# Moving a kernel's SBUF tiles from 64 and 96 bytes past a multiple of 128 to the multiple itself

## The chip, the cores and the metric

The kernel runs on one core of a Trainium2 chip. The time is the device time of one execution in microseconds; three executions gave 1589.37, 1592.58 and 1593.47 us, so the median is 1592.58. SBUF is the on-chip memory with 128 partitions; a tile `[P, D]` of float32 takes D × 4 bytes in every partition, at one and the same byte address in each. TensorE multiplies a stationary operand, which it loads first, with a moving operand, which it streams; it reads both from SBUF and writes to PSUM. This document is about the byte addresses at which these operands begin.

## What is computed

One decoder block on x of 1024 tokens by 1024 channels (`seq` = `D_MODEL` = 1024, one layer, one batch element), in float32:

```python
u = rms_norm(h, norm_mix); proj = u @ w_in
u_ssm, q, k, v, f_logit, gate_logits = split(proj)
y_ssm = gelu(s5_ssm(u_ssm, ...))                  # diagonal state-space branch, 512 wide
out_a = glu_a * sigmoid(glu_b)                    # from y_ssm @ w_glu
att = forgetting_attention(q, k, v, f_logit + b_forget)   # 8 heads of 64, causal
out_b = att @ w_fox_o
h = h + (gate_a * out_a + gate_b * out_b) @ w_mix_out
h = h + memory_cross_attention(rms_norm(h), rms_norm(mem), ...)   # 4 heads, 256 memory tokens
f_a, f_b = split(rms_norm(h, norm_ffn) @ w_ffn_in)
h = h + (silu(f_a) * f_b) @ w_ffn_out             # hidden width 2816
return rms_norm(h, norm_final)
```

## The kernel before

Every large product is made of three TensorE products. A float32 matrix is split into a high part (a cast to `float32r`, by ScalarE) and a low part (the rest, by VectorE); `split` (line 177) does it, and `mm3` (line 166) multiplies high by high, high by low and low by high into one PSUM bank. A matmul here has up to 128 rows, a stationary operand of mostly 128 columns and a moving operand of mostly 512 columns (2048 bytes in each partition); each has its own load of the stationary operand ahead of it.

The stages follow each other in the program: `stage_in` (norms, transposes, keys and values of the memory, the state-space input; its order is the hand-written string `ORDER_IN`), `stage_ssm` (gate products with the state-space branch between them), `Fox.run` (attention over eight heads, with the projections of later heads and the gated linear unit's products put between its score and value matmuls by hand-written slot tables), and `stage_tail` (the output products, cross-attention, and the feed-forward part, where seven products of half-size blocks replace eight). The order of the instructions is the order in which this code is written; nothing is planned at run time.

What decides the addresses is the allocation of the tile pools. Pools are laid out one behind the other in the order in which they are opened, and a tile's size is rounded up to 32 bytes. In this order stand: a few constants, `const` (identity, `mhalf`, `junk`), `small` (statistics of a few bytes), `wpool` with the weights as loaded (`raw`, two slots of `RAW` floats) and split (`whi`, `wlo`, four slots each of `WSLOT` floats), `big` (16 slots of 4096 bytes: the activations that are streamed), and behind it, one after another in the same place, the pools of the stages: `ssm` with `xin` or `qp` behind it, then `sh` (slots `half` of 2048 and `tmp` of 4096 bytes) with `fox` or `st2` behind it. So one small tile near the start moves everything behind it.

Three sizes matter to the change. `RAW` = 1072 and `SLOT` = 1040 (lines 31 and 32); `raw` holds at most 4 × 264 = 1056 floats, and `SLOT` is the size of the four `vhi` tiles of attention (line 1434), which hold two key blocks of 8 heads × 65 columns = 1040 floats. `msk` (line 1247) is the last tile of the pool `ssm`, 64 bytes, and `bfb` (line 1464) is a tile of 8 floats in `fox`, ahead of the attention tiles `hb`, `tri`, `trk`, `num`, `rb` and `pl`.

Where the operands of the matmuls begin, as the built program before has it (bytes past a multiple of 128):

| tiles | role on TensorE | past a multiple of 128 |
| --- | --- | --- |
| `whi`, `wlo`, all of `big`, `sh`, `st2` | moving and stationary, nearly all matmuls from the state-space stage on | 64 |
| `mT` (`mh`, `ml`), `xt` in `stage_in` | moving for the memory keys, stationary for its values | 96 |
| `qp` (state-space tables) and `hb0` to `hb3`, `pl` in `fox` | both, attention heads of odd number | 96 |
| `raw` | not read by TensorE | 64 and 0 |
| `vhi` | stationary, 65 columns from every 260 bytes | every multiple of 4 |
| `ident` | moving operand of the transposes | 0 |

The 264-column weights of the value projection (`values_of_v`, line 1445) lie four behind each other in one `whi` slot, 1056 bytes apart, so they begin at 64, 96, 0 and 32 past a multiple of 128, in this order.

Of the kernel before, what the change touches and what calls it, by code (L numbers as in the profile page):

```python
# [9 lines left out]
F32 = mybir.dt.float32  # L10
F32R = mybir.dt.float32r
# [8 lines left out]
P = 128  # L20
# [4 lines left out]
NH = 8  # L25
# [2 lines left out]
MH = 4  # L28
FH = 2816
EPS = 1e-6  # L30
SLOT = 1040
RAW = 1072

WSLOT = 1088
NEG = -1.0e30
# [31 lines left out]
def f32(ap):  # L67
    return ap.bitcast(F32)


class Act:


    def __init__(self, pool, tag, bufs, nk, n, kg=2, name="a"):
        self.kg, self.width = kg, D // kg

        def mk(s):
            return [[pool.tile([P, D], F32R, tag=tag, bufs=bufs, name=f"{name}{s}{k}_{h}")
                     .rearrange("p (k c) -> p k c", k=kg)
                     for h in range(n // self.width)] for k in range(nk // kg)]  # L80

        self.hi, self.lo = mk("h"), mk("l")
# [23 lines left out]
class Shared:  # L106
# [5 lines left out]
    def tmp(self, name, dt=F32):  # L112
        return self.pool.tile([P, D], dt, tag="tmp", bufs=4, name=name)
# [5 lines left out]
class Block:  # L119
    BANKS = {"mm": 3, "sc": 2, "pv": 2, "misc": 1}  # L120

    def __init__(self, ctx, tc):
        self.tc, self.nc = tc, tc.nc
        nc = self.nc
        self.V, self.A, self.G, self.T, self.S = nc.vector, nc.scalar, nc.gpsimd, nc.tensor, nc.sync
        self.const = ctx.enter_context(tc.tile_pool(name="const", bufs=1))
        self.small = ctx.enter_context(tc.tile_pool(name="small", bufs=3))
        self.wpool = ctx.enter_context(tc.tile_pool(name="wpool", bufs=4))
        self.dram = ctx.enter_context(tc.tile_pool(name="dram", bufs=1, space=DRAM))
        self.psum = ctx.enter_context(tc.tile_pool(name="psum", bufs=2, space=PSUM))  # L130
        self.ident = self.const.tile([P, P], F32, name="ident")
        make_identity(nc, self.ident)
        self.mhalf = self.const.tile([P, 1], F32, name="mhalf")
        nc.vector.memset(self.mhalf, -0.5)
        self.junk = self.const.tile([P, 512], BF16, name="junk")
        self.nbank = 0


    def bank(self, tag=None):
# [8 lines left out]
    def wload(self, pieces, cols, pool_lo=False, behind=None):  # L148

        raw = self.wpool.tile([P, RAW], F32, tag="raw", bufs=2, name="raw")  # L150
        for off, shape, src in pieces:
# [182 lines left out]
def stage_in(B, xp, s5, x, mem, g_mix, g_kv, w_in, w_mem_kv, uT, u_d, kv_d):  # L334
# [41 lines left out]
    def wget(i):  # L376
# [4 lines left out]
        else:  # L381
            src = w_in[:, C_U + (i - 8) * P:C_U + (i - 7) * P]
        raw[i] = B.wpool.tile([P, RAW], F32, tag="raw", bufs=2, name="raw")[:, :D]
        S.dma_start(raw[i].rearrange("p (k c) -> p k c", k=D // src.shape[-1]),
# [113 lines left out]
def stage_tail(B, big, s2, sh, x, glu, aT, gate_d, kv_d, w_fox_o, w_mix_out, g_mq, w_mem_q, w_mem_o, g_ffn,  # L498
# [57 lines left out]
    def wslots(src, pool_lo):  # L556

        nk = src.shape[0] // P
        raw = B.wpool.tile([P, RAW], F32, tag="raw", bufs=2, name="raw")[:, :D]
        S.dma_start(raw.rearrange("p (k c) -> p k c", k=nk), src.rearrange("(k p) c -> p k c", p=P))  # L560
# [241 lines left out]
    def w_fetch(j):  # L802
        raws[j] = B.wpool.tile([P, RAW], F32, tag="raw", bufs=2, name="raw")[:, :D], tmp("rawb")
        for r_, c in zip(raws[j], (0, FH)):
            f = S.dma_start(r_.rearrange("p (k c) -> p k c", k=8),
                            w_ffn_in[:, c + j * P:c + (j + 1) * P].rearrange("(k p) c -> p k c", p=P))
        return f
# [303 lines left out]
class S5:  # L1111
# [51 lines left out]
    def prepare(self):  # L1163
        B, sp, cT, bb, dbc, par = self.B, self.sp, self.cT, self.braw, self.dbc, self.par
# [76 lines left out]
        for i in range(2):  # L1241
            G.memset(self.cb[i], 0.0)
            for g in range(2):
# [4 lines left out]
        G.memset(msk, 1.0)  # L1248
        G.affine_select(out=msk, in_=msk, pattern=[[-1, 16]], compare_op=ALU.is_equal, fill=0.0, base=-112,
                        channel_multiplier=1)  # L1250
        self.dm = dbc.rearrange("p (g m) -> p g m", g=GRP)
        V.tensor_tensor(out=self.dm, in0=self.dm,
                        in1=msk.unsqueeze(1).to_broadcast([P, GRP, 16]), op=ALU.mult)
# [165 lines left out]
class Fox:  # L1419
# [11 lines left out]
    def prepare_v(self):  # L1431

        fp, G = self.fp, self.B.G
        self.vh = [fp.tile([P, SLOT], F32R, tag="vhi", bufs=4, name="vhi").rearrange("p (k h d) -> p k h d", k=2, h=NH)
                   for _ in range(4)]
        self.vl = [fp.tile([P, D], F32R, tag="vlo", bufs=4, name="vlo").rearrange("p (k c) -> p k c", k=2)
                   for _ in range(4)]
        for v_ in self.vh:
            G.memset(f32(v_[:, :, :, 64:65]), 1.0)
        self.fl = self.sh.half("fl")[:, :NT * NH].rearrange("p (t h) -> p t h", t=NT)  # L1440
        self.wv = {}
        for b, (c0, n) in ((1, (256, 264)), (0, (0, 256))):
            self.wv[b] = [self.B.wblock(self.w_in, 4 * kk, 4, C_V + c0, n, behind=self.B.ordered) for kk in range(2)]
# [17 lines left out]

    def log_forget(self):
        B, fp, V, S = self.B, self.fp, self.B.V, self.B.S
        bfb = fp.tile([P, NH], F32, name="bfb")
        S.dma_start(bfb, self.b_forget.partition_broadcast(P))
        both = self.sh.half("logf"), self.sh.half("logf")
        tmp = [t_[:, 64 * i:64 * i + 64] for t_ in both for i in range(8)]
        xl, ax, ee, s_, s2 = tmp[:5]
        V.tensor_tensor(out=xl.rearrange("p (t h) -> p t h", t=NT), in0=self.fl,
                        in1=bfb.unsqueeze(1).to_broadcast([P, NT, NH]), op=ALU.add)  # L1470
        V.tensor_scalar(out=ax, in0=xl, scalar1=-1.0, scalar2=None, op0=ALU.mult)
        V.tensor_tensor(out=ax, in0=ax, in1=xl, op=ALU.min)
        pp, sc = B.exp_parts(lambda s: tmp[5 + "xc k r p ib".split().index(s)], ax)
        V.scalar_tensor_tensor(out=ee, in0=pp, scalar=1.0, in1=sc, op0=ALU.add, op1=ALU.mult)

        V.tensor_scalar(out=s_, in0=ee, scalar1=2.0, scalar2=None, op0=ALU.add)
        V.reciprocal(s_, s_)
        V.tensor_mul(s_, s_, ee)
        V.tensor_mul(s2, s_, s_)
        V.tensor_scalar(out=ee, in0=s2, scalar1=1.0 / 17, scalar2=None, op0=ALU.mult)  # L1480
        for d in (15, 13, 11, 9, 7, 5, 3):
            V.scalar_tensor_tensor(out=ee, in0=ee, scalar=1.0 / d, in1=s2, op0=ALU.add, op1=ALU.mult)
        V.scalar_tensor_tensor(out=ee, in0=ee, scalar=1.0, in1=s_, op0=ALU.add, op1=ALU.mult)
        V.tensor_scalar(out=xl, in0=xl, scalar1=0.0, scalar2=None, op0=ALU.min)
        V.scalar_tensor_tensor(out=xl, in0=ee, scalar=-2.0, in1=xl, op0=ALU.mult, op1=ALU.add)
        self.logf = xl
# [42 lines left out]
    def project(self, h):  # L1529
# [5 lines left out]
        def load(behind=None):  # L1535
            src = lambda c: self.w_in[:, c + h * DH:c + (h + 1) * DH].rearrange("(k p) c -> p k c", p=P)
            raw = self.raw[h] = B.wpool.tile([P, RAW], F32, tag="raw", bufs=2, name="raw")[:, :D]
            rv = raw.rearrange("p (k c) -> p k c", k=8)
# [272 lines left out]
```

## Time and profile before

| | |
| --- | --- |
| time of an execution, median of 3 (lowest to highest) | 1592.58 us (1589.37 to 1593.47) |
| span of the profiled execution, first to last instruction | 1586.7 us |
| around the span, taken as median less span | 5.9 us |
| mean granted TensorE clock | 0.988 |
| matmuls | 7313, of which 5,844 with 512 columns |
| TensorE busy | 97% of the span |
| VectorE, ScalarE, GpSimd busy | 64%, 41%, 16% |
| DMA, mean | 152 GB/s |

The profile gives no own time for the profiled execution beside its span, so the 5.9 us between the span and the median stand for what lies around it. A row of the groups gives line, engine, operation, output tile <- input tiles, shape, count, then the busy time, the mean duration of one in ns, and the idle time ahead of it. Durations of matmuls overlap, since one starts while the last drains; how fast TensorE goes is read from the distance between two starts, in the view of the timeline, whose columns are start (us), duration (us), engine, line, operation.

### The profile page before, as it was taken

The page shows a single profiled execution, that of the slowest core. Times are in us where ns is not written, and L with a number is a line of the kernel's source. Part 1 is how long each engine was busy: PE and PEld are TensorE (multiplying, and loading weights), DVE is VectorE, ACT ScalarE, POOL GpSimd, SP SyncE. Part 2 cuts the span into 40 slices and gives each one's busy share as a digit, 9 for nine tenths or more (in the row PEclk, how much of TensorE's full clock was granted, in tenths as well). Part 3 has the DMA queues.
Part 4 walks back from the last instruction along what each step waited for, and adds up shares of the span by engine and source line. Part 5 has one row for each costly group of instructions (what it writes and reads, how often), then busy time and mean ns, then how long its engine had stood idle before and what let it go on. Part 6 is the DMA issues. An engine that isn't in the chain of part 4 may idle for free.

```text
span 1586.7 us, 20446 instructions
## 1 busy us (share of the span) xinstructions
PE 1534.0 (97%) x7313; PEld 1261.3 (79%) x7313; DVE 1019.5 (64%) x1850; ACT 655.2 (41%) x1173; POOL 254.3 (16%) x335
## 2 busy tenths in 40 slices
PE   7799999999999899999999999999999999999997
PEld 6578888898777668888888778888888888788885
DVE  6666445344688687675555697766677776565555
ACT  6422434323576553222435564333333333254342
POOL 2027653200212124110002200100000000000001
PEclk8899999999999999999999999999999999999999
DMA  7764445652023736357412186555444554796642
GB/s 266 125 132 80 127 131 110 130 145 30 18 52 48 186 95 208 125 172 259 160 46 75 54 283 239 170 164 163 155 153 160 166 162 156 261 391 223 195 150 106
DMA packets 197940, 240.86 MB, mean 152 GB/s; under 512 B 35448, under 2 KB 126488, under 8 KB 197328
## 3 DMA queue, kind: packets, MB, share of 16 engines
q1 hardware_dynamic: 191216, 223.84, 48.2%
q10 hardware_dynamic: 6624, 15.73, 2.6%
q8 instruction: 57, 0.93, 0.2%
q14 instruction: 43, 0.35, 0.1%
HBM read 165.60 MB, written 75.86 MB: 152 GB/s over the span
## 4 chain that ended last, share of the span: by engine, by line
PE 75%; DVE 8%; DMA 7%; issue 4%; POOL 3%; ACT 2%; SPq 1%; DVEq 0%; POOLq 0%; ACTq 0%
PE mm L868 14%; PE mm L168 7%; PE pv L868 7%; PE mm L170 7%; PE mm L169 7%; PE mm L1005 4%; PE sc L868 3%; PE sc L1005 3%; PE pv L1005 3%; PE sc L168 3%; PE sc L169 3%; PE sc L170 3%; DMA raw<-in_w_in_dram 2%; PE misc L1005 1%; PE pv L168 1%
## 5 line engine op out<-in xcount | busy, mean ns | idle before, releaser
L179 DVE TENSOR_TENSOR wlo<-raw,whi 128x1024 fp32r<-128x1024 f32 (+2 forms) x121 | 132.0, 1094 | 135.1 <-ACT whi L178 133.9
L178 ACT CAST whi<-raw 128x1024 fp32r<-128x1024 f32 (+2 forms) x124 | 116.1, 940 | 220.0 <-DMA raw<-in_w_ffn_in_dram 54.1
L168 PE MATMUL mm<-uh,whi 128*128 128x512 f32 x344 | 138.8, 404 | 2.8 <-ACT whi L178 2.7
L170 PE MATMUL mm<-uh,wlo 128*128 128x512 f32 x344 | 136.5, 397 | 1.7 <-DVE wlo L179 1.7
L169 PE MATMUL mm<-ul,whi 128*128 128x512 f32 x344 | 136.4, 396 | 0.0
L179 DVE TENSOR_TENSOR ol<-or,oh 128x1024 fp32r<-128x1024 f32 x73 | 89.3, 1224 | 71.6 <-ACT oh L178 70.3
L178 ACT CAST oh<-or 128x1024 fp32r<-128x1024 f32 x73 | 76.8, 1052 | 105.3 <-PE mm L1005 33.6
L900 POOL TENSOR_TENSOR g<-a,c 128x512 f32<-128x512 f32 x22 | 35.2, 1600 | 392.8 <-ACT a L899 373.9
L170 PEld LDWEIGHTS mm<-uh,wlo 128*128 128x128 f32 x344 | 65.7, 191 | 16.5 <-DVE wlo L179 3.1
L1630 POOL TENSOR_TENSOR pl<-pf,ph 128x512 fp32r<-128x512 f32 (+1 forms) x32 | 39.7, 1239 | 241.1 <-DVE ph L1629 196.1
L168 PEld LDWEIGHTS mm<-uh,whi 128*128 128x128 f32 x344 | 65.9, 192 | 15.5 <-ACT whi L178 3.2
L169 PEld LDWEIGHTS mm<-ul,whi 128*128 128x128 f32 x344 | 66.0, 192 | 11.3
L197 POOL TENSOR_TENSOR r<-ms,mhalf 128x1 f32<-128x1 f32 x26 | 15.1, 582 | 354.9 <-DVE ms L193 344.5
L1627 ACT ACTIVATE pf<-sc 128x512 f32<-128x512 f32 (+1 forms) x96 | 46.5, 490 | 46.3 <-DVE sc L1623 28.6
L868 PE MATMUL pv<-S3h,we 128*128 128x512 f32 x176 | 58.1, 389 | 0.0
L1633 DVE TENSOR_TENSOR pl<-pf,ph 128x512 fp32r<-128x512 f32 (+2 forms) x64 | 35.1, 550 | 10.2 <-ACT ph L1632 9.5
L1005 PE MATMUL mm<-oh 128*128 128x512 f32 x106 | 41.2, 389 | 0.0
L1005 PE MATMUL mm<-ol,oh 128*128 128x512 f32 x106 | 41.2, 389 | 0.0
L1005 PE MATMUL mm<-oh,ol 128*128 128x512 f32 x106 | 41.2, 389 | 0.0
L168 PE MATMUL mm<-yh,whi 128*128 128x512 f32 x104 | 40.9, 393 | 0.0
L168 PE MATMUL sc<-uh,whi 128*128 128x512 f32 x104 | 40.8, 393 | 0.0
L170 PE MATMUL mm<-yh,wlo 128*128 128x512 f32 x104 | 40.6, 390 | 0.0
(580 smaller groups left out, 4537.5 us busy)
## 6 DMA issues: line engine op xcount, KB each, us to landing
or<-c_d SPq DMA_DIRECT2D x77, 256.0 KB
raw<-in_w_in_dram SPq DMA_DIRECT2D x22, 512.0 KB
wo<-in_w_ffn_out_dram SPq DMA_DIRECT2D x22, 512.0 KB
c_d<-g SPq DMA_DIRECT2D x44, 256.0 KB
t_d<-wo SPq DMA_DIRECT2D x44, 256.0 KB
or<-t_d SPq DMA_DIRECT2D x44, 256.0 KB
raw<-in_w_ffn_in_dram SPq DMA_DIRECT2D x20, 512.0 KB
rawb<-in_w_ffn_in_dram SPq DMA_DIRECT2D x20, 512.0 KB
```

The lines of the kernel that those rows point to most:

```text
L168: T.matmul(ps, lh, rh, start=first, stop=False)
L169: T.matmul(ps, lh, rl, start=False, stop=False)
L170: T.matmul(ps, ll, rh, start=False, stop=last)
L178: self.A.copy(hi, src)
L179: (self.G if pool_lo else self.V).tensor_sub(lo, src, f32(hi))
L197: self.G.tensor_tensor(out=r, in0=v, in1=self.mhalf[:, 0:n], op=ALU.pow)
L868: T.matmul(ps, l_[:, k, :], r_, start=first and k == 0 and i == 0, stop=k == 3 and i == 2, skip_group_check=True)
L900: G.tensor_mul(g[:, 512:], a1, c1)
L1005: T.matmul(ps, l_[:, gi], r_[:, 512:], start=n < 3 and p == 0 and k == 0 or n == 7 and p == 0 and k == 0, stop=p == NP - 1 and k == 2, ski ...
L1627: self.exp = A.activation(pf[:, off:], ps[:, off:], AF.Exp)
L1630: G.tensor_sub(pl[:, off:], pf[:, off:], f32(ph[:, off:]))
L1633: V.tensor_sub(pl[:, off:], pf[:, off:], f32(ph[:, off:]))
```

## The change

The change puts two unused tiles, `pad`, into pools, changes two sizes, and makes one tile longer.

- `RAW` from 1072 to 1056 floats: 64 bytes less in each of two slots.
- A pad of 64 bytes at the end of `const`. Together with `RAW`, everything from `whi` on begins 64 bytes lower, at 0 past a multiple of 128 instead of 64; `raw` begins at 0 in both slots.
- A pad of 96 bytes behind `msk` in `ssm`, so that `xin` and `qp` behind it begin at 0 instead of 96.
- `SLOT` from 1040 to 1056 floats, with a view of the first 1040, so that all four `vhi` slots begin at 0 (before: 64 and 0 by turns), and `vlo` behind them.
- `bfb` gets 64 floats (256 bytes) instead of 8 (32 bytes), so that what follows it in `fox` begins at 0 instead of 96.

```diff
-SLOT = 1040
-RAW = 1072
+SLOT = 1056
+RAW = 1056
...
         self.junk = self.const.tile([P, 512], BF16, name="junk")
+        self.pad(self.const, 64)
         self.nbank = 0
+
+    def pad(self, pool, nbytes):
+
+        pool.tile([P, nbytes // 4], F32, name="pad")
...
         G.affine_select(out=msk, in_=msk, pattern=[[-1, 16]], compare_op=ALU.is_equal, fill=0.0, base=-112,
                         channel_multiplier=1)
+        B.pad(sp, 96)
...
-        self.vh = [fp.tile([P, SLOT], F32R, tag="vhi", bufs=4, name="vhi").rearrange("p (k h d) -> p k h d", k=2, h=NH)
+        self.vh = [fp.tile([P, SLOT], F32R, tag="vhi", bufs=4, name="vhi")[:, :1040].rearrange("p (k h d) -> p k h d", k=2, h=NH)
...
-        bfb = fp.tile([P, NH], F32, name="bfb")
+        bfb = fp.tile([P, 64], F32, name="bfb")[:, :NH]
```

In the built program after, all the tiles of the table above that were at 64 or 96 are at 0. The distance between a weight slot and an activation tile, both of which moved by 64, is what it was. Still off a multiple of 128 are the 65-column pieces of `vhi` (a head is 260 bytes) and three of the four 264-column weight pieces, now at 0, 32, 64 and 96. The same instructions stand in the same order on every engine; the pads are never written or read. One thing is added beside the addresses: the first cast into each of the four `vhi` tiles, on ScalarE at the start of attention, now also waits for GpSimd, whose memset of the same tile's 65th columns (line 1439) the cast did not wait for before. ScalarE's instructions there, from the last weight cast of the stage before on (`gs` is a gate's sigmoid, `gate_d` its place in DRAM, `sc` and `mm` are PSUM banks; the name behind waits is the engine or DMA queue waited for), before:

```order
L178 CAST whi<-raw 128x1024 [waits DMAHW5_49,PE_49]
L471 ACTIVATE gs<-mm 128x512 [waits DMAHW4_49,PE_49]
L472 DMA gate_d<-gs 128x512 [waits Activation_49]
L1457 CAST vhi<-sc 128x4x64 [waits PE_49]
L1457 CAST vhi<-mm 128x4x64 [waits PE_49] x2
```

and after:

```order
L183 CAST whi<-raw 128x1024 [waits DMAHW5_49,PE_49]
L476 ACTIVATE gs<-mm 128x512 [waits DMAHW4_49,PE_49]
L477 DMA gate_d<-gs 128x512 [waits Activation_49]
L1463 CAST vhi<-sc 128x4x64 [waits PE_49,Pool_49]
L1463 CAST vhi<-mm 128x4x64 [waits PE_49]
L1463 CAST vhi<-mm 128x4x64 [waits PE_49,Pool_49]
```

The casts stand where they stood; every second one has a second thing to wait for.

## The prediction

> **What bounds the kernel.** First the busy times and the chain of the page, then the windows by stage, then the timeline inside stages, since the change concerns how fast TensorE reads.
>
> ```profile
> PE 1534.0 (97%) x7313; PEld 1261.3 (79%) x7313; DVE 1019.5 (64%) x1850; ACT 655.2 (41%) x1173; POOL 254.3 (16%) x335
> ...
> PE 75%; DVE 8%; DMA 7%; issue 4%; POOL 3%; ACT 2%; SPq 1%; DVEq 0%; POOLq 0%; ACTq 0%
> ```
>
> ```profile
> 0.00:100.00 100.00, 79.74 (x392) 65.44 (x393) 73.99 (x241) 48.45 (x83) 14.62 (x16) 0.88 0.72 181
> 100.00:320.00 220.00, 218.45 (x1110) 185.69 (x1109) 107.47 (x152) 79.47 (x124) 106.25 (x209) 1.00 0.52 117
> ...
> 400.00:600.00 200.00, 190.42 (x908) 142.12 (x907) 153.49 (x370) 121.97 (x233) 39.65 (x32) 0.99 0.37 86
> 600.00:800.00 200.00, 200.00 (x901) 165.66 (x900) 131.65 (x173) 63.46 (x109) 31.60 (x22) 1.00 0.54 176
> ...
> 1000.00:1300.00 300.00, 300.00 (x1326) 248.39 (x1325) 213.92 (x303) 106.61 (x173) 25.35 (x16) 1.00 0.50 161
> 1300.00:1587.00 287.00, 273.39 (x1204) 225.40 (x1202) 167.77 (x214) 110.08 (x140) 11.53 (x12) 0.99 0.61 210
> ```
>
> From 100 to 320 us and from 600 us to the end TensorE hardly waits, and 75% of the chain is its work: there the time is the number of matmuls times the distance between two starts. In the first 100 us and in attention (320 to 600 us) other engines and transfers end part of the waits. So the question is one number: the distance between starts. In the chain by time, a dense stretch of the feed-forward part reads:
>
> ```profile
> 1031.52 5.44 PE mm L868 x24
> 1050.56 5.44 PE mm L868 x24
> ```
>
> 24 matmuls of 512 columns take 5.44 us, 226.7 ns each. What would be the least? While the clock is granted at a half, 256 columns take 0.43 / 2 = 0.215 us, and the stream is just the columns, at the rate of the half clock:
>
> ```profile
> 20.20 0.41 PE L168 MATMUL mm<-mh,whi 128*128 128x256 f32 x1
> 20.42 0.41 PE L169 MATMUL mm<-ml,whi 128*128 128x256 f32 x1
> 20.63 0.41 PE L170 MATMUL mm<-mh,wlo 128*128 128x256 f32 x1
> ```
>
> ```profile
> 19.50:21.00 1.50, 1.50 (x9) 1.50 (x8) 1.36 (x5) 0.74 (x1) 0.00 (x0) 0.50 0.98 370
> ```
>
> At the full clock 512 columns should then take as long, about 213 ns. So each wide matmul carries about 13 ns beyond its columns. That surplus is all that the change can win or enlarge: there are 5,844 matmuls of 512 columns, 4,906 of them in the two dense windows (counted in the timeline), so **one ns on the distance is worth 4.9 us there**.
>
> **Does the surplus come from the place modulo 128?** The program before already streams and loads from several places, and the rows compare them. First the moving operand. The 264-column products of the value projection take their weights from 64, 96, 0 and 32 past a multiple of 128, three matmuls each, with the stationary operand at 64 throughout. The starts of these groups of three, and of the next group at 64:
>
> ```profile
> 323.32 0.29 PE L168 MATMUL mm<-whi,uh 128*128 128x264 f32 x1
> ...
> 323.69 0.28 PE L168 MATMUL mm<-whi,uh 128*128 128x264 f32 x1
> ...
> 324.05 0.29 PE L168 MATMUL mm<-whi,uh 128*128 128x264 f32 x1
> ...
> 324.42 0.28 PE L168 MATMUL mm<-whi,uh 128*128 128x264 f32 x1
> ...
> 324.78 0.29 PE L168 MATMUL mm<-whi,uh 128*128 128x264 f32 x1
> ```
>
> The groups take 0.37, 0.36, 0.37 and 0.36 us: 120 to 123 ns a matmul, with the group at 0 no shorter than the one at 64. Their columns alone are 264 / 512 × 213 = 110 ns, so all four places carry 10 to 13 ns.
>
> The memory keys stream 256 columns from 96, at the full clock, with the stationary operand at 64:
>
> ```profile
> 23.56 0.28 PE L168 MATMUL mm<-mh,whi 128*128 128x256 f32 x1
> ...
> 24.15 0.28 PE L170 MATMUL mm<-mh,wlo 128*128 128x256 f32 x1
> ```
>
> Five distances in 0.59 us are 118 ns, or 11 ns beyond 107. If a stream were read in whole lines of 128 bytes, 32 columns each, 256 columns from 96 would touch nine lines and take 120. More against lines are 128 columns from 64:
>
> ```profile
> 560.43 0.22 PE L1645 MATMUL pv<-ph,vhi 128*65 128x128 f32 x1
> 560.49 0.22 PE L1646 MATMUL pv<-ph,vlo 128*64 128x128 f32 x1
> 560.55 0.28 PE L1652 MATMUL pv<-pl,vhi 128*65 128x256 f32 x1
> ```
>
> Five lines would be 5 × 13.3 = 67 ns; the starts lie 60 apart. For lines speaks that 226.7 ns is 17 of them, and 512 columns from 64 touch just 17.
>
> Then the stationary operand. `vhi` begins at every multiple of 4 bytes, yet its loads are alike (the columns are lowest/median/highest ns):
>
> ```profile
> L1645 PEld LDWEIGHTS pv<-ph,vhi x96: 133/135/183, 400.1 to 604.8; 128*65 128x65 f32 x96
> ```
>
> The pair of places does matter in one row. The memory's values stream from 64 while loading from 96:
>
> ```profile
> 34.61 0.39 PE L169 MATMUL sc<-wlo,mh 128*128 128x512 f32 x1
> ...
> 36.47 0.40 PE L168 MATMUL sc<-whi,mh 128*128 128x512 f32 x1
> ```
>
> Eight distances in 1.86 us are 233 ns, 6 more than with both at 64. The Trainium skill, "TensorE: Matmul & The Clock Gate", section "Step-by-step: what each phase is for", says that streaming and loading have separate read ports and that a load steals nothing from a running matmul; by it the pair could not matter. The row disagrees, unless something else sets 233.
>
> **The change part by part.** *Dense windows, 100 to 320 and 600 to the end.* Both operands go from 64 to 0. Their distance is unchanged, and the moving operand's own place showed between 0 and −1 ns from 64 to 0. The bounds: nothing left of the surplus, −13 ns × 4,906 = −64 us; or the pair's bad case, 233 for 227, +6 × 4,906 = +29 us. I take 0, by the 264-column groups, the only row with a moving operand at 0 in this format.
>
> *Attention.* Here operands at 64, 96 and anywhere (`vhi`) alternate. All rows but the last below are 512 wide:
>
> ```profile
> 563.20 0.40 PE L1621 MATMUL sc<-hb 128*128 128x512 f32 x1
> 563.43 0.40 PE L1645 MATMUL pv<-ph,vhi 128*65 128x512 f32 x1
> ...
> 565.76 0.34 PE L1620 MATMUL sc<-hb 69*128 69x384 f32 x1
> ```
>
> Eleven distances in 2.56 us are 233 ns, the pair's bad value. After the change all but `vhi` agree. 751 such matmuls lie in 320 to 600 us: up to 6 × 751 = 4.5 us of TensorE, at least 0 (among the eleven, L1621 at 563.20 has both operands at 64 already and is followed 0.23 us later). Part is covered by waits; I take −1.5 us.
>
> *First 100 us.* Values from 233 to 227: 48 × 6 = −0.3 us. Keys from 118 to at most the 123 of the 264-column group: 96 × 5 = +0.5, mostly under transfers (DMA 0.72 of the window). Sum 0.
>
> *The four new waits.* The awaited memsets are over long before the first cast:
>
> ```profile
> L1457 ACT CAST vhi<-sc x6: 373/373/377, 323.5 to 378.0; 128x256 fp32r<-128x256 f32 x6
> ...
> L1439 POOL MEMSET vhi<- x4: 123/128/129, 301.5 to 309.9; 128x16 f32 x4
> ```
>
> They end by 310.1, 13 us ahead of 323.5: 0. If that cover went, the cast would hold ScalarE's next instructions and VectorE's `vlo`; a memset is 0.13 us, so the cost is at most 0.5 us in all.
>
> *Other engines.* The casts of `wdh` read `raw` at 64 and at 0 by turns:
>
> ```profile
> L178 ACT CAST wdh<-raw x20: 607/615/617, 982.8 to 1340.6; 128x512 fp32r<-128x512 f32 x20
> ```
>
> All lie within 10 ns, so ScalarE is taken at 0. No row separates transfers by place; DMA is 7% of the chain, 111 us, and a change of 2% either way is ±2 us. I take 0, between them. `bfb`, the pads and the longer `vhi` slots are no work.
>
> The sum is −1.5 us on the span of 1586.7, or 1585.2. The median of the runs is 5.9 above the span; with it, **1591 us**.
>
> **Rivals.** *The surplus goes.* If 17 lines are the cause, 16 remain: 213 ns. 13 × 4,906 = 64 us, and half of 751 × 15 in attention, 6 us: 1593 − 70 = **1523**; if a third of the surplus stays, 1546. For it is the coincidence of 17; against it the 60 ns and the 264-column group at 0. It decides if the distance at 1031 us falls under 222. The Trainium skill, the page named above, section "Back-to-back issue gap", gives N/2.4 + 2.5 ns, 216 for 512, naming no condition on the place: by it the surplus is an anomaly that something must cause, and without it an estimate by that page is 1533. Here no row of 512 columns shows 216.
>
> *The pair locks at 64 and not at 0: slower.* In the dense windows 227 is exact throughout; where it isn't reached, 233 stands. If 227 needs the present places, all 4,906 go to 233: +29, and the time is **1622**. For it: the value row. Against it: the distance of the operands doesn't change. It decides from a distance of 228 on, which is +5 us.
>
> *A small gain or loss.* A surplus that shifts by 1 to 4 ns, as among the four groups: 5 to 20 us either way, so 1573 to 1588, or 1598 to 1613.
>
> *The change doesn't do what it says*, since `vhi` and three in four of the 264-column pieces stay off; but these are under 400 matmuls, and only the attention term would shrink to 0: 1593.
>
> **How the numbers follow.** Within 0.3% (4.8 us, about what measurement tells from no change): 0.37, the case of my sum, the last rival in it. The surplus gone, wholly or by half, 1523 to 1558: 0.25. A small gain: 0.12. A small loss: 0.14. The pair unlocked: 0.12. So faster 0.37, slower 0.26. The likeliest case alone spans 1588 to 1597. The range, 1525 to 1608, takes in nearly all of the surplus and the smaller losses, and leaves out the unlocked pair and the largest small losses, under 0.2.
>
> **What would show it.** Right: 24 matmuls at about 1031 us still take 5.44 us, and the windows hold the same counts. The lines: 5.1 to 5.3 us instead. The pair: 5.6. Attention: the eleven distances under 2.56 us. Most likely to make me wrong is that no row has both operands at 0, and the price of a ns is high.

## The result, and the profile after

The changed kernel takes 1591.57 us (median of 14 executions, 1588.37 to 1594.28), the kernel before in the same session 1591.07 us (14 executions, 1587.65 to 1594.01). The ratio is 0.9999 with a 95% interval of 0.999 to 1.0008: no difference that the measurement can tell.

The page of the changed kernel, busy times and shares of the chain:

```profile
PE 1538.2 (97%) x7313; PEld 1264.9 (80%) x7313; DVE 1020.5 (64%) x1850; ACT 656.3 (41%) x1173; POOL 254.9 (16%) x335
...
PE 73%; DVE 9%; DMA 7%; issue 5%; POOL 3%; ACT 2%; SPq 1%; DVEq 0%; POOLq 0%; ACTq 0%
```

The windows by stage (us, then busy time and number of instructions of TensorE, its loads, VectorE, ScalarE, GpSimd, then the granted clock, DMA share and GB/s):

```profile
0.00:100.00 100.00, 80.64 (x396) 66.09 (x397) 74.78 (x243) 48.70 (x83) 15.20 (x17) 0.88 0.73 183
100.00:320.00 220.00, 218.00 (x1100) 185.43 (x1099) 106.43 (x150) 79.63 (x124) 105.18 (x209) 0.99 0.52 117
...
600.00:800.00 200.00, 200.00 (x898) 165.49 (x897) 131.16 (x174) 63.52 (x107) 32.74 (x22) 1.00 0.56 180
...
1000.00:1300.00 300.00, 300.00 (x1325) 248.39 (x1324) 215.46 (x304) 109.02 (x176) 25.30 (x16) 1.00 0.49 158
```

From 1000 to 1300 us TensorE does 1325 matmuls; before, it did 1326. From 100 to 320 us it does 1100 instead of 1110, mainly since in this execution the clock was granted at a half for 3.4 us of that window (from 190.2 us; mean 0.99 against 1.00 before). The chain by time shows the dense stretch of the feed-forward part:

```profile
1034.20 5.44 PE mm L873 x24
1053.24 5.44 PE mm L873 x24
```

24 matmuls take 5.44 us, as they did: 226.7 ns each, at 0 past a multiple of 128 bytes as at 64. The profiled span is 1587.9 us, 1.2 us above that of before, which is within what single executions differ by.

### The profile page after: what moved, and what is told of

Its sections match the earlier page's. It is cut to its first block, busy times and chain, and to the rows that moved or that the text cites. A ratio compares the mean times of both kernels' runs of the same rounds, so it can differ in the third digit from the quotient of the medians.

```text
span 1587.9 us, 20450 instructions
## 1 busy us (share of the span) xinstructions
PE 1538.2 (97%) x7313; PEld 1264.9 (80%) x7313; DVE 1020.5 (64%) x1850; ACT 656.3 (41%) x1173; POOL 254.9 (16%) x335
## 4 chain that ended last, share of the span: by engine, by line
PE 73%; DVE 9%; DMA 7%; issue 5%; POOL 3%; ACT 2%; SPq 1%; DVEq 0%; POOLq 0%; ACTq 0%
PE mm L873 14%; PE pv L873 7%; PE mm L173 6%; PE mm L175 6%; PE mm L174 6%; PE mm L1010 4%; PE sc L873 3%; DMA raw<-in_w_in_dram 3%; PE sc L1010 3%; PE pv L1010 3%; PE sc L173 3%; PE sc L174 3%; PE sc L175 3%; PE misc L1010 1%; PE pv L173 1%
## 5 line engine op out<-in xcount | busy, mean ns | idle before, releaser
L1105 POOL TENSOR_TENSOR sg<-sg,ga 128x512 f32<-128x512 f32 x16 | 29.4, 1863 | 73.3 <-DVE sg L1098 73.3
```

The lines of the kernel that those rows point to most:

```text
L1105: self.B.G.tensor_mul(self.out[j][:, cs], self.out[j][:, cs], ga)
```

## Experiments

Two addresses are compared below: the byte at which a matmul's moving tile begins, and the byte of the stationary tile that is loaded while it streams, which is the one the next matmul uses. **Distance** is the first less the second, and the runs soon made it necessary to count it modulo 256. Inside a product both stationary tiles mostly begin at the same place, so counts over a whole kernel are given for a matmul's own stationary tile unless the loaded one is named. The addresses are those of the built programs. Distances between starts ("ns" below) are differences of neighbouring start times in the trace, averaged; breaks above 260 ns are left out. A series has settled when its distances repeat to the end.

### A bench of places

Ahead of the kernel's own work, 35 configurations of 28 matmuls stream from one resident tile. `m` and `s` are the bytes by which the moving and the stationary tile are moved; at `m` = `s` = 0 both begin 64 past a multiple of 256, as the weights and most activations of the kernel before do.

```diff
+    for m, s, n, w, half in BENCH:
+        ps = B.bank("misc")
+        src, z = (h_, 2) if half else (t_, 4)
+        for i in range(28):
+            B.T.matmul(ps[0:w, :n], src[:, (4608 + s) // z:(4608 + s) // z + w],
+                       src[:, m // z:m // z + n], start=True, stop=True)
```

> The kernel before with a stretch of 35 configurations ahead of its own work, each 28 matmuls back to back from one resident tile into one PSUM bank; they differ in the place of the moving tile and of the stationary tile modulo 128 bytes, in columns, in stationary width and in type; the rest of the kernel is as before. Three theories. N (the place does not matter, the 13 ns that a 512-column matmul takes beyond its columns belong to the operation): about 227 ns from start to start for every place with 512 float32r columns, 128 wide. D (only the difference between the two places counts): 227 ns where both are equal modulo 64 or 128 bytes, about 233 ns or more at differences of 16, 32, 48 and 96, the same for a moved moving tile as for a moved stationary one. P (each tile's own place counts): the configurations with both tiles moved alike by 32 or 64 bytes differ from the first by 3 ns or more. The bf16 rows and those with narrower stationary tiles tell what the 13 ns belong to: 213 to 216 ns in bf16 if they belong to the 4-byte type, an unchanged 227 ns if they belong to any matmul.

The chain by time, a row for each configuration of 28: moving tile moved by 32, 64, 128 and 256 bytes; both moved by 64, by 16; and bf16:

```profile
40.80 6.74 PE misc L305 x28
...
54.42 6.63 PE misc L305 x28
...
81.43 6.79 PE misc L305 x28
...
95.11 6.66 PE misc L305 x28
...
136.09 6.66 PE misc L305 x28
...
156.22 6.81 PE misc L305 x28
...
206.63 6.22 PE misc L305 x28
```

Each row of the 4-byte type holds one break of about 0.1 us at its start, and the first matmuls of a series differ, so the settled end of a series is compared. It repeats exactly: 227, 226, 227 ns for 256 and for both moved by 64 (mean 226.7); 233.3 for 32; 228.9 for 64; 232.8 for 128. Moving the stationary tile by 128 gives 232.7, like moving the other; by 32, 64 and 96 it gives 233.2, 233.4 and 234.4. Both moved by 32, 64 or 96: 226.7. Theory N falls, and so does P for moves by 32 and 64 bytes. D holds for places that are multiples of 32 bytes, but with a period of **256** bytes: 128 apart is a poor distance, 256 apart the best one again, and a move of the moving tile by 192 (233.4) equals one of the stationary tile by 64 (233.4). With both moved by 16 bytes it is 233.3 at distance 0, so off multiples of 32 the place itself counts too.

In bf16 all three places give 215.8 ns. With a stationary tile of 64 columns the 4-byte matmul took 230 ns, with 32 columns 232. So the surplus belongs to the 4-byte type, and a smaller stationary tile does not take it away.

### One pad between weights and activations: 32, 64 and 128 bytes

```diff
+    shift = ctx.enter_context(tc.tile_pool(name="shift", bufs=1))
+    shift.tile([P, 8], F32, name="pad")          # 16 for 64 bytes, 32 for 128
     big = ctx.enter_context(tc.tile_pool(name="big", bufs=16))
```

In 3,528 matmuls the operands come to stand at another distance. Those whose two operands both lie behind the pad keep distance 0 in the same program, chiefly three of the seven feed-forward products, whose weights `wdh` and `we` are combined into tiles behind it, and the output products, whose operands are the two halves of one slot.

> The kernel before with one 32-byte pad between the weights and the activations: in 3,528 of the 5,844 matmuls of 512 columns the moving tile begins 32 bytes (3,144 of them) or 96 bytes (384) off the place of the stationary one modulo 128, where both stood alike; the products into the feed-forward's second half keep equal places. Theory N: the time within 0.3% of before, 1586 to 1596 us, and 227 ns in every dense window. Theory D: 227 becomes about 233 ns in those 3,528, which is 3,528 x 6.3 ns = 22 us, so about 1613 us, with 227 ns left in the matmuls whose two places stay alike. Theory P: slower or faster by more than 5 us, and by as much as with both moved alike.

> As with the 32-byte pad, with 64 bytes between: the weights stay at 64 and the activations begin at 0 modulo 128, a difference of 64 bytes in the same 3,528 matmuls. Theory N: within 0.3% of before, 1586 to 1596 us. Theory D with a period of 128 bytes: about 1613 us as with 32; D with a period of 64: no change. Theory P: by what moving the activations alone from 64 to 0 is worth; the changed kernel moved both and showed no change, so P would need the two to cancel.

> The kernel before with a 128-byte pad between the weights and the activations: every tile begins where it began modulo 128 bytes, and in 3,528 of the 5,844 matmuls of 512 columns the distance between the two is 128 modulo 256. If only places modulo 128 count (the words of the change, and the reading of the prediction): within 0.3% of before, 1586 to 1596 us. Theory D256: 232.8 ns instead of 226.7 in those 3,528, which is 21 us, so about 1610 us.

| pad, bytes | time, us (before in the same session) | ratio, 95% interval | settled distance between starts, ns |
| --- | --- | --- | --- |
| 32 | 1608.55 (1590.85) | 1.0105 [1.0084, 1.0127] | 233.3 |
| 64 | 1597.02 (1590.85) | 1.0046 [1.003, 1.0062] | 228.9, and 233.3 where weights stream |
| 128 | 1608.31 (1590.14) | 1.0097 [1.0072, 1.0123] | 232.5 |

The chain by time in the feed-forward part, 32 bytes:

```profile
1028.24 5.60 PE mm L870 x24
1033.84 2.79 PE sc L870 x12
1036.63 2.72 PE mm L870 x12
```

64 bytes:

```profile
1019.57 5.49 PE mm L870 x24
```

and 128 bytes:

```profile
1026.56 5.58 PE mm L870 x24
1032.14 2.79 PE sc L870 x12
1034.93 2.72 PE mm L870 x12
```

In one stretch of one program, the `sc` product at the new distance takes 2.79 us for 12, 232.5 ns on average, and the `mm` product behind it, whose distance is still 0, takes 2.72 us, 226.7 ns. The bench's price is the kernel's price. The ends of products also tell which stationary tile counts. In the dense windows of the 32-byte kernel, 47 matmuls of unbroken series stand at distance 0 from their own tile and at 32 from the one that is loaded while they stream: they take 235.0 ns. Another 49 stand the other way round and take 227.8. It is the tile being loaded. Counted by that tile, the dense windows of the 32-byte kernel have 2,894 matmuls at a changed distance: × 6.6 ns = 19 us, against 17.7 measured. For 128 bytes 2,894 × 5.8 = 17 us, against 18.2 by the medians and 11.4 to 19.6 by the interval of the ratio. For 64 bytes 2,509 × 2.2 and 385 × 6.6 are 8.1 us, against 6.2 by the medians and 4.8 to 9.9 by the interval. The expectation of 21 to 22 us had counted all 3,528 and so those in the first 100 us and in attention too. For 64 bytes neither form of D was right: a period of 128 said 1613 us and a period of 64 no change, and the price lies between.

The third kernel leaves every address as it was modulo 128 and is 1% slower; theory D256 had said about 1610 us. Modulo 128 is the wrong measure.

### Everything moved together by 32 bytes

```diff
         self.const = ctx.enter_context(tc.tile_pool(name="const", bufs=1))
...
+        self.const.tile([P, 8], F32, name="pad")
```

> The kernel before with a 32-byte pad ahead of everything that TensorE reads: weights and activations begin 96 bytes past a multiple of 128 where they began at 64, and the two stay alike. Theories N and D: within 0.3% of before, 1586 to 1596 us, 227 ns in the dense windows. Theory P: the dense windows leave 227 ns by 1 ns or more, that is by 5 us or more.

1589.16 us against 1590.85, ratio 0.9988 [0.9976, 0.9999]: within 0.3%, and the chain in the dense stretch reads as before:

```profile
1012.01 5.44 PE mm L869 x24
1017.45 2.72 PE sc L869 x12
```

With both at 96 past a multiple of 128, TensorE does what it does at 64 and at 0. Theory P falls for the places that this kernel's tiles can have, since its pools round to 32 bytes.

### The bench, finer

```diff
-BENCH = [(0, 0, 512, 128, 0), (4, 0, 512, 128, 0), ...]      # 35, of 28 matmuls
+BENCH = [(m, 0, 512, 128, 0) for m in range(0, 256, 4)]      # 102 in all, of 24 matmuls
+     + [(4, 4, ...), (8, 8, ...), (48, 48, ...), (128, 128, ...), (144, 32, ...), (128, 16, ...)]
+     + [(m, 0, 256, 128, 0) for m in range(0, 256, 16)] + [(m, 0, 264, 128, 0) for m in range(0, 256, 16)]
```

> The same bench with 102 configurations of 24 matmuls: the moving tile's place in steps of 4 bytes over 256 bytes for 512 float32r columns, in steps of 16 for 256 and for 264 columns, and six pairs with both tiles moved. Theory D256 (the distance from the stationary tile's place to the moving tile's counts, with a period of 256 bytes, as far as places are multiples of 32): 226.7 ns at distance 0 and near it at 112, 228.9 at 64, 232 to 234 at 32, 96, 128 and 192; the pairs with equal distance and places that are multiples of 32 give what their distance gives alone: 226.7 for 128 and 128, 226.7 for 144 and 32. If some distance leaves no collision at all, it shows as less than 226 ns, down to the 216 ns that bf16 took. Theory N is gone after the first bench; a theory that the pairs of the first bench differ by chance (each has one run of 28) would give other values at the same distances now, apart by 2 ns or more.

The chain by time, rows for the moving tile moved by 20, 32, 64 and 128, and for both moved by 128:

```profile
41.50 5.96 PE misc L305 x24
...
59.21 5.86 PE misc L305 x24
...
106.35 5.81 PE misc L305 x24
...
200.86 5.87 PE misc L305 x24
...
408.03 5.76 PE misc L305 x24
```

| distance modulo 256 | 0 | 32 | 64 | 96 | 128 | 160 | 192 | 224 |
| --- | --- | --- | --- | --- | --- | --- | --- | --- |
| 512 columns, settled ns | 226.7 | 233.3 | 228.9 | 233.3 | 232.7 | 234.3 | 233.3 | 233.2 |
| 256 columns | 120.0 | 116.5 | 117.7 | 119.9 | 118.6 | 117.3 | 113.3 | 118.2 |
| 264 columns | 121.4 | 121.7 | 119.9 | 126.7 | 123.3 | 121.9 | 120.0 | 119.9 |

Of the 64 places for 512 columns none settles below 226.7 ns, and the worst (20, 116, 132, 228 and 244) settle at 240.0. So nothing is to be had below 226.7 by placing, and distance 0 is the best of those the kernel's pools can give. Which distance is best depends on the number of columns: with 256 columns 0 is, with 96, the worst of the eight.

The pairs with both tiles moved agree with the expectation where both places are multiples of 32 (226.7 for 128 and 128), and 144 and 32 give the 226.7 of 112 alone. Off them the distance does not suffice: 128 and 16, also 112 apart, settle at 233.3, and both moved by 4, 8 or 48 give 237.8, 231.1 and 230.0 at distance 0.

The rival, that values differ by chance, is right for some places off multiples of 32: 48 settled at 230.0 in the first bench and at 233.3 here, 112 at 226.7 in both benches and at 231.2 in the next one. A series can settle in more than one pattern. At the multiples of 32 both benches and the dense windows of the kernels agree within 0.5 ns for 512 columns.

### Broken runs

```diff
+    for pattern, reps in BENCH:            # e.g. [(0, 0, 512, 128)] * 3 + [(0, 0, 256, 128)], 8 times
+        ps = B.bank("misc")
+        for i in range(reps):
+            for m, s, n, w in pattern:
+                B.T.matmul(ps[0:w, :n], t_[:, (4608 + s) // 4:(4608 + s) // 4 + w],
+                           t_[:, m // 4:m // 4 + n], start=True, stop=True)
```

> The same bench with repeated patterns in place of 24 equal matmuls: runs of 1, 2, 3, 4, 6 and 12 matmuls of 512 columns at distance 0, each run followed by one or two of other columns or a narrow stationary tile, as attention mixes them; some patterns at distance 112, 240, 32 and 128. In the first benches an unbroken series at distance 0 took 6 to 11 matmuls of 224 to 236 ns before it settled at 226.7, and at 112 and 240 it settled at once. Theory S (attention reads 231 ns at distance 0 because its runs are broken before they settle): the 512-column matmuls of the patterns with runs of 1 to 4 take 230 to 234 ns on average at distance 0, those with runs of 12 about 229 or less, and runs of 3 at distance 112 and 240 nearer 227. Rival (the surplus of attention is made elsewhere, by waits and the work of other engines): the patterns take 227 ns at distance 0 whatever the length of the run.

The chain by time, rows for an unbroken series of 24; eight times three wide and one of 256 columns; three times twelve wide and one of 256; six times three wide and four of 264:

```profile
12.27 5.48 PE misc L304 x24
...
29.30 6.68 PE misc L304 x32
...
51.56 8.80 PE misc L304 x39
...
156.12 7.27 PE misc L304 x42
```

The wide matmuls of the pattern with runs of three take 224, 231 and 236 ns over and over (230.2 on average), with runs of one 236.7, two 232.1, four 231.5, six 230.5. In runs of twelve they begin at 233, 236, 228, 233, 230 and are at 227 from the sixth on. Theory S is right on most runs at distance 0, with two misses beside the 236.7. Runs of three with four matmuls of 264 columns behind them take 226, 226 and 227 ns from the third time on, so a short run need not be slow; and runs of two with one narrow stationary tile take 229.2. S is wrong on 112 and 240: runs of three take 230 and 231 there, no nearer 227, so no distance is known that spares short runs.

The kernel's own attention window holds the same test, since some unbroken series stand in it. One of the changed kernel, in the timeline (start, duration, engine, line, operation):

```profile
591.77 0.39 PE L1627 MATMUL sc<-hb,hb 128*128 128x512 f32 x1
...
592.47 0.39 PE L175 MATMUL mm<-yh,wlo 128*128 128x512 f32 x1
...
594.51 0.39 PE L175 MATMUL mm<-yh,wlo 128*128 128x512 f32 x1
```

By the unrounded starts the first three distances are 231, 232 and 231 ns; the nine behind them take 2.04 us, 226.7 each. The other engines are as busy in this stretch as in one of short runs, where the distance is 233 ns (columns as in the windows above, first the short runs):

```profile
566.10:568.70 2.60, 2.60 (x12) 1.77 (x12) 2.35 (x6) 1.88 (x3) 1.30 (x1) 1.00 0.04 11
591.70:594.60 2.90, 2.90 (x14) 2.38 (x14) 2.39 (x3) 2.17 (x4) 1.29 (x1) 1.00 0.21 47
```

### The memory values at distance 0

```diff
         with tc.tile_pool(name="xin", bufs=1) as xp:
+            xp.tile([P, 56], F32, name="pad")
             stage_in(B, xp, s5, x, mem, norm_mix[0], norm_mem_kv[0], w_in, w_mem_kv, uT, u_d, kv_d)
```

> The kernel before with a 224-byte pad ahead of the tiles of the input stage, so that its normalised tiles stand at distance 0 modulo 256 from their weights, as all other 128-wide products but the 264-column pieces do: 48 matmuls of 512 columns go from distance 224 to 0, and 96 of 256 columns from 32 to 0. Theory D256: the 512-column matmuls of the memory values, 232.3 ns on average in the first 100 us of the kernel before, come down to 227 to 229 ns; 48 x 4 ns = 0.2 us, in a stage where TensorE waits for a fifth of the time anyway, so the time stays within 0.3% of before. Rival (the values read 233 ns for another reason, their short runs or the traffic of that stage): they stay at 232 ns.

1589.90 us against 1591.44, ratio 0.9999 [0.9985, 1.0013]. The timeline in the stage of the values (start, duration, engine, line, operation):

```profile
34.27 0.39 PE L169 MATMUL sc<-wlo,mh 128*128 128x512 f32 x1
...
35.66 0.39 PE L169 MATMUL sc<-wlo,mh 128*128 128x512 f32 x1
...
36.57 0.39 PE L170 MATMUL sc<-whi,ml 128*128 128x512 f32 x1
```

The first six distances take 1.39 us, 232 ns each, the next four 0.91 us, 227 each by the unrounded starts (226, 227, 227 and 226): the run settles as the bench's did, which no run of the values does in the kernel before or the changed one. On average over the 48 the distance comes down only from 232.3 to 230.3 ns, less than the 227 to 229 expected, since the runs break after 3 to 12. Both sides were half right. The keys, 256 columns wide, go from distance 32 to 0 and from 117.3 to 120.1 ns, as the bench's 116.5 and 120.0 have it: with this width distance 0 is not the good one.

## Why the prediction was right, and where it was not

**The time.** The forecast of 1591 us lies 0.6 from the measured 1591.57, and part of that is luck. It started from a median of three executions, 1592.58, where 14 gave 1591.07, and took off 1.5 us for attention that did not come. The interval of the ratio, from −1.6 to +1.3 us, holds −1.5 and 0 alike, so only the traces can judge the terms. The 5.9 us between span and median are not what lies around the span, either: the profiled execution of the changed kernel took 1589.97 us with a span of 1587.9, so 2.1 lie around it, and the rest was the spread of executions.

**Dense windows, 0.** Right, in time and in reason: the distance of the operands is what it was, and a tile's own place does nothing as long as both move together. Before and after, 5,652 of the 5,844 wide matmuls stand at distance 0 modulo 256, the best value; a move of one operand alone costs 6 to 18 us in the runs above.

**The pair of places.** The step read 233 ns in the values as the price of 64 against 96 modulo 128, and concluded that equal places would bring 227. Half of it stands: the pair does decide, and the runs show 226.7 to 234.4 ns by the distance alone. The Trainium skill, "TensorE: Matmul & The Clock Gate", section "Step-by-step: what each phase is for", says that a load takes nothing from a running matmul; these runs differ from it. The period was wrong. The values stood 224 apart modulo 256 before and stand 128 apart after, both poor. The timeline of the changed kernel:

```profile
34.52 0.39 PE L174 MATMUL sc<-wlo,mh 128*128 128x512 f32 x1
...
36.84 0.40 PE L175 MATMUL sc<-whi,ml 128*128 128x512 f32 x1
```

Ten distances in 2.32 us are 232 ns, with both operands at 0 modulo 128; over all 48 it is 232.7 against 232.3 before. The term of −0.3 us for them did not come, for this reason. The keys went from distance 32 to 128, and from 117.3 to 119.1 ns, +0.2 us over the 96 within the +0.5 allowed.

**Attention, −1.5 us.** This is the term that failed. It put attention's 233 ns to the same pair. The prediction named its sign: the eleven distances from 563.20 us on, 2.56 us before, should come under that. The same eleven after the change:

```profile
566.15 0.40 PE L1627 MATMUL sc<-hb 128*128 128x512 f32 x1
...
568.71 0.34 PE L1626 MATMUL sc<-hb 69*128 69x384 f32 x1
```

They take 2.56 us, 233 ns each. Over the 751 wide matmuls of 320 to 600 us the average is 231.4 ns before and 231.7 after. What failed is the premise that a poor pair makes the 233. Of the 751, 471 stream before, and 575 after, while a 128-column tile at distance 0 is loaded, and those 471 read 231.1 ns on average already. The 104 that the change did bring from 224 or 32 to 0 gained nothing: 92 of them run without a break in both traces and take 233.6 ns before, 233.9 after. What the runs show in place of the pair is that runs here end before they settle. Short runs at distance 0 read 230 to 237 ns in most patterns of the broken-run bench. In attention itself, before, the average over runs at distance 0 with 128-column loads falls from 232.1 ns in the first five distances to 226.7 from the eleventh on. The work of other engines is not needed to explain it, as the series at 591.77 us shows. Nor is a lower clock: before, the window has one stretch of 3.4 us at a half (from 525 us), whose distances of over 400 ns are left out as breaks. Why a series takes so long to settle is open.

**The other columns.** The 264-column pieces now stream from 0, 32, 64 and 96 instead of 64, 96, 0 and 32. The starts of the groups of three:

```profile
324.60 0.29 PE L173 MATMUL mm<-whi,uh 128*128 128x264 f32 x1
...
324.97 0.28 PE L173 MATMUL mm<-whi,uh 128*128 128x264 f32 x1
...
325.33 0.29 PE L173 MATMUL mm<-whi,uh 128*128 128x264 f32 x1
...
325.70 0.28 PE L173 MATMUL mm<-whi,uh 128*128 128x264 f32 x1
...
326.05 0.29 PE L173 MATMUL mm<-whi,uh 128*128 128x264 f32 x1
```

0.37, 0.36, 0.37 and 0.35 us against 0.37, 0.36, 0.37 and 0.36: the pattern stayed with the order of the pieces, whose distance to the stationary operand (0, 32, 64, 96) is what it was, while their own places changed. Over all 48 matmuls of each piece the averages before and after agree within 0.1 ns. The prediction's reading, that the place of the moving operand alone shows nothing, is borne out.

**The four new waits and the other engines, 0.** Right. The tile view of `vhi` after, and the casts of `wdh`, which now always read `raw` at 0:

```profile
L1463 ACT CAST vhi<-sc x7: 372/373/377, 324.9 to 400.7; 128x256 fp32r<-128x256 f32 x7
L1445 POOL MEMSET vhi<- x4: 126/128/130, 302.4 to 311.2; 128x16 f32 x4
```

```profile
L183 ACT CAST wdh<-raw x20: 608/615/617, 985.5 to 1343.3; 128x512 fp32r<-128x512 f32 x20
```

The memsets are over 13 us before the first cast, and the casts take the 615 ns of before. Transfers are 7% of the chain before and after, so the 0 taken for them shows no error.

**The rivals.** The surplus that goes with a seventeenth line: refuted by the changed kernel itself, 226.7 ns with 16 lines as with 17, and by the bench, where no place goes below 226.7. The Trainium skill, "TensorE: Matmul & The Clock Gate", section "Back-to-back issue gap", gives 216 ns for 512 columns. The bench's 215.8 in bf16 agrees with it; the 226.7 of float32r does not, at any place tried. The pair that locks at 64 and not at 0: refuted, it locks at 64, 96 and 0 alike. Its price (6 ns a matmul) was real, but it is paid when the distance changes. The prediction named the unchanged distance as what spoke against this rival, and that decided. That the change does not do what it says is nearest in its number, attention at 0, but not in its reason: matmuls that came to distance 0 gained nothing either. The change aligned places whose alignment does not matter, and left nearly all distances where they were.

## What to carry to other kernels

For streams of 512 columns of 4-byte operands, look at the distance between the moving tile and the stationary tile loaded under it, modulo 256 bytes, before looking at either address; a stray 32-byte tile between the weights and the activations cost this kernel 1.05%. A dense stretch tells at once whether the pair is at its best: 24 matmuls of 512 columns take 5.44 us at distance 0, and 5.5 to 5.6 at 64, 32 and 128. For other widths measure it, since 256 columns have other good distances. When a row is explained by two places, a bench of a few dozen series separates "which place" from "which distance" and finds the period.

## What the runs showed that was not expected

- The period of 256 bytes, and that 128 apart (232.7 ns) is no better than 32 apart (233.3). What lies behind it is open.
- Series of 4-byte matmuls that settle to one value do so at whole multiples of 3.33 ns, the time of 8 columns (8 / 512 of 213 ns): 226.7, 230.0, 233.3 and 240.0 ns for 512 columns (68, 69, 70 and 72 of them), 113.3, 116.7 and 120.0 for 256 (34, 35 and 36), 126.7 for 264 (38).
- A series at distance 0 takes 3 to 11 distances to settle, and a single matmul of 256 columns unsettles it. In attention this costs about 4 ns in each wide matmul (231.1 against 226.7), 3 us over the 751 of them; no placing tried here gets it back.
